# Order of the weight loads around the head outputs' read-back, in a two-layer attention and convolution trunk

## The chip, the cores and the metric

The kernel runs on one core of a Trainium2 chip. The metric is the device time of one execution in microseconds. Before the change three runs took 2350.84, 2352.64 and 2359.91 us; the median is 2352.64.

## The reference

Two layers of a diffusion trunk, over 512 latent tokens and 256 context tokens of width 1024. In each layer the tokens are normed and modulated, and one projection gives a convolution's input, queries, keys, values and gates. A convolution branch and a differential attention (8 heads, two softmax maps each) are projected, gated and merged, and a squared-ReLU MLP follows. Context tokens read only context tokens, and the last layer leaves their own update out. The part around the change:

```python
w = p[:, :, 0] - lam * p[:, :, 1]
out = rmsnorm(einsum('bhqk,bkhv->bqhv', w, vals), sub_g) * (1 - lam_init)   # per head
...
y_conv = conformer_conv(conv_in, ...) @ w_conv_out
y_attn = attn @ w_attn_out
g = sigmoid(gate_logits + b_gate)
return (g_conv * y_conv + g_attn * y_attn) @ w_out
```

The modulation is `silu(c) @ w_ada + b_ada`, six vectors of 1024 for the latent tokens and six for the context.

## The kernel before

All matrices are held with channels on the 128 partitions. To keep float32 accuracy each operand is split into a rounded half and a remainder (`split`, L75: ScalarE rounds at L76, VectorE or GpSimd subtracts at L77), and each product is three matmuls (`mm3`, L109 to L111: rounded by rounded, rounded by remainder, remainder by rounded).

Weights come in slabs of 256 columns, 1 MB each (`load_slab`, L84): a transfer on SyncE's queue (L90) into a tile of the tag `raw`, then the split, half a slab at a time, into the tags `whi` and `wlo`, two buffers each. In the stretch in question `raw` has two buffers, and the modulation's slabs (`ada_slab`, L217, transfer at L81) use the same two. A modulation slab needs no split: sixteen small matmuls (L224), a copy, two transposes (L233) and three small VectorE instructions. Layer 0 has 24 modulation slabs, of which 4 to 8 stand beside each stage; layer 1's were worked out earlier, in layer 0's MLP.

The attention writes each head's unnormed output to memory (`at_d`, L770) and, at its end, all the heads' scales (`rs_d`, L817). Both are read back: `branch_load` (L976) reads one latent head, or two context heads, into a tile `ar` of tag `t2k`, four buffers (L981), and its scales, spread over all partitions, into a tile `arb` of tag `ar`, three buffers (one transfer per head, L984); VectorE multiplies (L986). The loop at L1072 splits the product into `hh` and `hl` (`h1h` and `h1l` in the trace), in which the gates' input stood till then. Layer 0 has twelve such loads, eight latent heads and four pairs of context heads; layer 1 has the eight latent ones. The first four are traced ahead of the last gate slab.

The loop at L1077 then multiplies the heads by `w_attn_out`: four slabs, for each the load `wao`, in layer 0 also modulation slab 16 + s, then the matmuls `ya` of the latent and the context tokens (L1086). The layer norm of the convolution runs in pieces between the slabs.

The order on each engine is not the order of the code. A planner at build time takes instructions by their place in the code as their inputs and buffers come free in its own model of time, and writes each engine's list, which the chip runs in that order. `tc.issue_after(x)` adds an edge without a wait: what the block puts on `x`'s engine stands behind `x` in that engine's list, and nothing waits for `x` to finish.

Of the kernel before, what the change touches and what calls it, by code (L numbers as in the profile page):

```python
# [14 lines left out]
P = 128  # L15
# [36 lines left out]
def trunk_kernel(  # L52
# [6 lines left out]
    nc = tc.nc  # L59
# [15 lines left out]
    def split(hi, lo, src, lo_eng=None):  # L75
        nc.scalar.activation(out=hi, in_=src, func=AF.Copy)  # L76
        return (lo_eng or nc.vector).tensor_tensor(out=lo, in0=src, in1=f32(hi), op=ALU.subtract)  # L77

    def raw_slab(src, name):
        r = state["tp"].tile([P, KT, 256], F32, tag="raw", name=name, bufs=state["nraw"])  # L80
        nc.sync.dma_start(r, src)  # L81
        return r

    def load_slab(src, name, shape=(KT, 256), lo_eng=None):  # L84
        r = state["tp"].tile([P, *shape], F32, tag="raw", name=f"r_{name}", bufs=state["nraw"])
        if isinstance(src, (list, tuple)):
            for dst, s in src:
                nc.sync.dma_start(r[:, :, dst], s)
        else:
            state["load"] = nc.sync.dma_start(r, src)  # L90
        hi = wpool.tile([P, *shape], F32R, tag="whi", name=f"h_{name}")
        lo = wpool.tile([P, *shape], F32R, tag="wlo", name=f"l_{name}")
        half = shape[0] // 2
        engs = lo_eng if isinstance(lo_eng, tuple) else (lo_eng, lo_eng)
        with ExitStack() as behind:
            for ins in state["behind"]:
                behind.enter_context(tc.issue_after(ins))
            for n, (k, eng) in enumerate(zip((slice(0, half), slice(half, shape[0])), engs)):
                if n and state["turn"]:
                    behind.enter_context(tc.issue_after(state["turn"]))  # L100
                split(hi[:, k], lo[:, k], r[:, k], eng)
        return hi, lo

    def rows(src, col0, ncols):
        return src[:, col0 : col0 + ncols].rearrange("(k p) n -> p k n", p=P)
# [7 lines left out]
    def fm_block(ps, w, m0, a, toks, nk=KT, lo_last=False):  # L113

        if lo_last:
            for k in range(nk):
                for j in range(2):
                    nc.tensor.matmul(ps, w[j][:, k, m0 : m0 + P], a(k)[0][:, toks],
                                     start=k + j == 0, stop=False)
            for k in range(nk):  # L120
                nc.tensor.matmul(ps, w[0][:, k, m0 : m0 + P], a(k)[1][:, toks],
                                 start=False, stop=k == nk - 1)
            return
        for k in range(nk):
            mm3(ps, (w[0][:, k, m0 : m0 + P], w[1][:, k, m0 : m0 + P]),
                (a(k)[0][:, toks], a(k)[1][:, toks]), k == 0, k == nk - 1)
# [14 lines left out]
    rs_d = [dpool.tile([H, SEQ if i == DEPTH - 1 else NT], F32, name=f"rs_d{i}")  # L141
            for i in range(DEPTH)]

    state = {"behind": (), "turn": None}
# [72 lines left out]
    def ada_slab(i, L, s):  # L217

        mi = state["mi"]
        r = raw_slab(rows(w_ada[i], 256 * s, 256), f"ada{i}_{s}")  # L220
        ps = mi(f"adaps{i}_{s}")
        for k in range(KT):
            j = k % 4
            nc.tensor.matmul(ps[32 * j : 32 * j + 32, :256], cvec[:, k, :], r[:, k, :],  # L224
                             start=k < 4, stop=k >= 4, tile_position=(0, 32 * j))
        if state["nt"] == 3:
            sb = state["tp"].tile([P, 512], F32, tag="t2k", bufs=3, name=f"adasb{i}_{s}")[:, :256]
        else:
            sb = spool.tile([P, 512], F32, tag="dg", name=f"adasb{i}_{s}", bufs=1)[:, :256]
        nc.scalar.activation(out=sb, in_=ps[:, :256], func=AF.Copy)  # L230
        pc = ps[:, 256:512]
        for m in range(2):
            nc.tensor.transpose(pc[:, m * P : m * P + P], sb[:, m * P : m * P + P], ident)  # L233
        ad = L["ad"][:, :, 2 * s : 2 * s + 2]
        for q in range(2):
            nc.vector.tensor_reduce(
                out=ad[:, q], in_=pc.rearrange("p (m j r) -> p m j r", m=2, j=4)[:, :, :, q],
                axis=AX.X, op=ALU.add)
        nc.vector.tensor_tensor(
            out=ad, in0=ad,  # L240
            in1=L["cols"][:, R_BADA + 2 * s : R_BADA + 2 * s + 2].unsqueeze(1)
            .to_broadcast([P, 2, 2]),
            op=ALU.add)
# [126 lines left out]
    for t in range(NTT):  # L370
# [4 lines left out]
        if t == 1:  # L375
            L = layer_params(0)
# [72 lines left out]
    for i in range(DEPTH):  # L449
# [370 lines left out]
        def drain(gen):  # L820
            for _ in gen:
                pass
# [113 lines left out]
        def ps_for(g, name):  # L936
            if g.start:
                return mc.tile([P, 512], F32, tag="mc", name=name)
            return mm_tile(name)
# [28 lines left out]
        def some_taps(n):  # L968
            for _ in range(n):
                next(tap, None)  # L970
# [5 lines left out]
        def branch_load(h, g):  # L976
            W = g.stop - g.start
            per = 512 // W
            r = gp.tile([P, 512], F32, tag="t2k", bufs=4,
                        name=f"ar{i}_{h}_{g.start}").rearrange("p (h d) -> p h d", h=per)  # L980
            nc.sync.dma_start(r, at_d[i][h : h + per, :, g].rearrange("h p d -> p h d"))  # L981
            rb = gp.tile([P, 512], F32, tag="ar", bufs=3, name=f"arb{i}_{h}_{g.start}")
            for j in range(per):
                nc.sync.dma_start(rb[:, j * W : j * W + W],  # L984
                                  rs_d[i][h + j, g].partition_broadcast(P))
            nc.vector.tensor_tensor(out=r, in0=r, in1=rb.rearrange("p (h d) -> p h d", h=per),  # L986
                                    op=ALU.mult)
            ready.append(r)
# [3 lines left out]
        for half, lst in ((1, ga), (0, gc)):  # L992
            for s in range(4):
                if (half, s) not in wg:
                    gate_slab(half, s)
                if half == 0 and s == 3:
                    for hg in branch[:4]:
                        branch_load(*hg)
                w = wg.pop((half, s))
                for m in range(2):  # L1000
                    mb = 2 * s + m
                    t = g3(f"g{i}_{half}_{mb}")
                    lst[mb] = t
                    for g in groups:
                        W = g.stop - g.start
                        ps = ps_for(g, f"gt{i}_{half}_{mb}_{g.start}")
                        fm_block(ps[:, :W], w, m * P, lambda k: (hh[:, k], hl[:, k]), g)
                        bcol = R_BG + half * KT + mb
                        nc.scalar.activation(out=t[:, g], in_=ps[:, :W], func=AF.Sigmoid,
                                             bias=cols[:, bcol : bcol + 1])  # L1010
                    some_taps(per_gate)
                    if m == 0 and not state.get("ada_done"):
                        ada_slab(i, L, 8 + 4 * half + s)
# [61 lines left out]
            (h, g), r = branch.pop(0), ready.pop(0)  # L1075
            split(ah[:, h : h + r.shape[1], g], al[:, h : h + r.shape[1], g], r)
        for s in range(4):  # L1077
            w = load_slab(rows(w_attn_out[i], 256 * s, 256), f"wao{i}_{s}")
            if not state.get("ada_done"):
                ada_slab(i, L, 16 + s)  # L1080
            for g in groups:
                W = g.stop - g.start
                for m in range(2):
                    mb = 2 * s + m
                    ps = ps_for(g, f"ya{i}_{mb}_{g.start}")
                    fm_block(ps[:, :W], w, m * P, lambda k: (ah[:, k], al[:, k]), g)  # L1086
                    nc.vector.tensor_tensor(out=ga[mb][:, g], in0=ga[mb][:, g], in1=ps[:, :W],
                                            op=ALU.mult)
                    if last and (s, m) == (3, 0):
                        next(ln, None)  # L1090
                if s < 1 + last:
                    some_taps(per_ya)
            if s == last:
                drain(tap)
                ln = layer_norm()
            if s >= last:
                next(ln, None)
# [10 lines left out]
        for s in range(2):  # L1108
            state["behind"] = normed if s else ()
            w = load_slab(w_conv_out[i][:, 512 * s : 512 * s + 512]  # L1110
                          .rearrange("(k p) n -> p k n", p=P), f"wco{i}_{s}", shape=(CT, 512))
# [4 lines left out]
            for m in range(4):  # L1116
                mb = 4 * s + m
                for g in groups:
                    W = g.stop - g.start
# [186 lines left out]
        if not last:  # L1306
# [3 lines left out]
            L = Ln  # L1310
# [77 lines left out]
```

## Time and profile before

| | |
|---|---|
| median of three runs | 2352.64 us |
| profiled execution | 2353.61 us, span 2351.8 us |
| TensorE busy | 2276.6 us (97%) |
| VectorE, ScalarE, GpSimd busy | 1476.0, 995.2, 687.3 us |
| DMA | 224.76 MB, mean 96 GB/s |
| granted clock of TensorE, mean | 0.988 |

The span is the time from the first to the last instruction of the program; the profiled execution took 1.8 us more. In the rows, PE is TensorE, DVE is VectorE, ACT is ScalarE and SPq is SyncE's queue; L12 is line 12 of the kernel. `out<-in` names tiles without their numbers: `ar<-at_d` is a read of a head's output, `arb<-rs_d` one of its scales, `r_wao` an attention-output slab, `ada` a modulation slab. A transfer's row has the time that its issue took; the time to landing stands apart. The stage of the change lies from about 600 to 690 us in layer 0 and from about 1865 to 1910 us in layer 1.

### The profile page before, as it was taken

What the parts mean: (1) busy time and instruction counts of PE and PEld (TensorE: products, weight loads), DVE (VectorE), ACT (ScalarE), POOL (GpSimd) and SP (SyncE); (2) the same over time, 40 slices, a digit from 0 to 9 for tenths busy, and PEclk for the clock granted to TensorE, in tenths of its full rate; (3) what the DMA queues carried; (4) which work ended last, traced back from release to release, by engine and by line L of the source; (5) the groups of instructions that cost most, each with busy time, mean ns of one, the idle gap of its engine ahead of it and who ended that gap; (6) DMA issues with size and microseconds to landing.
All of it is one profiled execution on the core that took longest, in us unless ns stands there. A gap on an engine that the chain in (4) does not pass through costs nothing.

```text
span 2351.8 us, 36393 instructions
## 1 busy us (share of the span) xinstructions
PE 2276.6 (97%) x14626; PEld 2042.8 (87%) x14626; DVE 1476.0 (63%) x2587; ACT 995.2 (42%) x1965; POOL 687.3 (29%) x790
## 2 busy tenths in 40 slices
PE   7999999999999999999999999999899999999999
PEld 6999998888888988888888988999877879888887
DVE  6777776699656455565655465767759966433332
ACT  5556654522332362332415255655542334432432
POOL 1866764100000133232223266757610000000000
PEclk9999999999999999999999999999999999999999
DMA  9111111143535124333343211111114323223222
GB/s 313 57 42 34 44 46 44 46 160 125 180 119 175 51 81 127 115 128 115 113 130 127 89 46 57 44 43 44 61 59 141 112 90 126 90 90 98 99 90 72
DMA packets 222570, 224.76 MB, mean 96 GB/s; under 512 B 6256, under 2 KB 212544, under 8 KB 222272
## 3 DMA queue, kind: packets, MB, share of 16 engines
q1 hardware_dynamic: 222400, 222.43, 29.4%
q8 instruction: 115, 1.88, 0.3%
q14 instruction: 55, 0.45, 0.1%
HBM read 208.73 MB, written 13.67 MB: 95 GB/s over the span
## 4 chain that ended last, share of the span: by engine, by line
PE 83%; DVE 7%; ACT 4%; POOL 2%; DMA 2%; issue 1%; SPq 0%; ACTq 0%; POOLq 0%; DVEq 0%
PE r L109 6%; PE r L110 6%; PE r L111 6%; PE f L110 6%; PE f L109 6%; PE f L111 6%; PE gt L109 3%; PE gt L110 3%; PE gt L111 3%; PE qk L109 2%; PE qk L110 2%; PE qk L111 2%; PE v L109 2%; PE v L110 2%; PE v L111 2%; PE o L109 2%
## 5 line engine op out<-in xcount | busy, mean ns | idle before, releaser
L110 PE MATMUL f<-h2l,h_w 128*128 128x512 f32 (+1 forms) x832 | 284.5, 343 | 1.1 <-POOL h2l L77 1.1
L109 PE MATMUL f<-h2h,h_w 128*128 128x512 f32 (+1 forms) x832 | 282.9, 343 | 2.2 <-ACT h2h L76 1.7
L111 PE MATMUL f<-h2h,l_w 128*128 128x512 f32 (+1 forms) x832 | 283.0, 342 | 0.0
L109 PE MATMUL r<-fh,h_w 128*128 128x512 f32 (+1 forms) x832 | 283.0, 341 | 0.0
L110 PE MATMUL r<-fl,h_w 128*128 128x512 f32 (+1 forms) x832 | 282.9, 340 | 0.0
L111 PE MATMUL r<-fh,l_w 128*128 128x512 f32 (+1 forms) x832 | 282.8, 340 | 0.0
L77 POOL TENSOR_TENSOR l_w<-r_w,h_w 128x1024 fp32r<-128x1024 f32 x64 | 157.8, 2487 | 339.5 <-ACT h_w L76 339.5
L76 ACT ACTIVATE h_w<-r_w 128x1024 fp32r<-128x1024 f32 x128 | 128.6, 1052 | 254.3 <-PE r L110 117.2
L959 DVE SCALAR_TENSOR_TENSOR cacc<-z,cols,cacc 128x783 f32<-128x783 f32 (+1 forms) x240 | 201.2, 891 | 0.3
L279 DVE SCALAR_TENSOR_TENSOR adaac<-ar,cvec,adaac 128x256 f32<-128x256 f32 x336 | 160.8, 541 | 44.6 <-DMA ar<-in_w_ada_dram 22.7
L109 PE MATMUL qk<-h_wqk,h1h 128*128 128x256 f32 x640 | 183.3, 289 | 0.7 <-ACT h1h L76 0.7
L1154 DVE SCALAR_TENSOR_TENSOR X<-r,ad,X 128x512 f32<-128x512 f32 (+1 forms) x104 | 65.1, 625 | 189.0 <-PE r L111 188.8
L110 PE MATMUL qk<-l_wqk,h1h 128*128 128x256 f32 x640 | 180.6, 284 | 0.0
L111 PE MATMUL qk<-h_wqk,h1l 128*128 128x256 f32 x640 | 176.9, 285 | 0.3 <-POOL h1l L77 0.3
L726 DVE TENSOR_REDUCE st<-S 128x1 f32<-128x768 f32 (+1 forms) x160 | 134.7, 846 | 66.8 <-PE S L724 65.3
L109 PEld LDWEIGHTS f<-h2h,h_w 128*128 128x128 f32 x832 | 158.1, 191 | 21.1 <-ACT h2h L76 2.3
L110 PEld LDWEIGHTS f<-h2l,h_w 128*128 128x128 f32 x832 | 159.1, 191 | 19.6 <-POOL h2l L77 1.9
L111 PEld LDWEIGHTS f<-h2h,l_w 128*128 128x128 f32 x832 | 158.8, 191 | 17.7
L111 PEld LDWEIGHTS r<-fh,l_w 128*128 128x128 f32 x832 | 157.7, 190 | 17.7
L109 PEld LDWEIGHTS r<-fh,h_w 128*128 128x128 f32 x832 | 157.7, 190 | 17.4
L110 PEld LDWEIGHTS r<-fl,h_w 128*128 128x128 f32 x832 | 157.8, 190 | 17.2
L1235 DVE TENSOR_TENSOR fl<-fr,fh 128x512 fp32r<-128x512 f32 (+1 forms) x104 | 67.9, 659 | 138.4 <-ACT fr L1234 138.2
(255 smaller groups left out, 6297.7 us busy)
## 6 DMA issues: line engine op xcount, KB each, us to landing
r_w<-in_w_mlp_dram SPq DMA_DIRECT2D x64, 1024.0 KB, 5.4
ada<-in_w_ada_dram SPq DMA_DIRECT2D x24, 1024.0 KB, 6.1
ar<-in_w_ada_dram SPq DMA_DIRECT2D x48, 512.0 KB, 3.5
r_wqk<-in_w_in_dram SPq DMA_DIRECT2D x32, 512.0 KB, 5.1
r_wg<-in_w_in_dram SPq DMA_DIRECT2D x16, 1024.0 KB, 5.9
r_wv<-in_w_in_dram SPq DMA_DIRECT2D x8, 1024.0 KB, 5.2
r_wao<-in_w_attn_out_dram SPq DMA_DIRECT2D x8, 1024.0 KB, 4.8
r_wo<-in_w_out_dram SPq DMA_DIRECT2D x8, 1024.0 KB, 7.3
```

What stands on the lines that cost most here:

```text
L76: nc.scalar.activation(out=hi, in_=src, func=AF.Copy)
L77: return (lo_eng or nc.vector).tensor_tensor(out=lo, in0=src, in1=f32(hi), op=ALU.subtract)
L109: nc.tensor.matmul(ps, sh, mh, start=first, stop=False)
L110: nc.tensor.matmul(ps, sh, ml, start=False, stop=False)
L111: nc.tensor.matmul(ps, sl, mh, start=False, stop=last)
L279: nc.vector.scalar_tensor_tensor(out=a[:, q], in0=r[:, j], scalar=cvec[:, k, q : q + 1], in1=a[:, q], op0=ALU.mult, op1=ALU.add)
L726: nc.vector.tensor_reduce(out=st[:, m : m + 1], in_=S[:, :nkey], axis=AX.X, op=ALU.max, negate=True)
L959: nc.vector.scalar_tensor_tensor(out=ca[cc][:, :CV], in0=zt[cc][:, t : t + CV], scalar=wcol, in1=ca[cc][:, :CV], op0=ALU.mult, op1=ALU.add)
L1154: state["done"] = nc.vector.scalar_tensor_tensor(out=X[:, mb, g], in0=ps[:, :W], scalar=gate[:, s, mb : mb + 1], in1=X[:, mb, g], op0=ALU. ...
L1235: state["done"] = nc.vector.tensor_tensor(out=fl[mb][:, g], in0=r[:, :W], in1=f32(fh[mb][:, g]), op=ALU.subtract).ins
```

## The change

The last transfer of scales is remembered. In the loop over the four attention-output slabs, slab 1's transfer is placed behind it on SyncE's queue, and so are the modulation slabs 16 and 17 that stand beside slabs 0 and 1. In layer 1, which has no modulation slabs left, it is slab 1 alone. The edge holds for the transfers only, because no other instruction of the blocks runs on SyncE.

```diff
             for j in range(per):
-                nc.sync.dma_start(rb[:, j * W : j * W + W],
-                                  rs_d[i][h + j, g].partition_broadcast(P))
+                state["back"] = nc.sync.dma_start(rb[:, j * W : j * W + W],
+                                                  rs_d[i][h + j, g].partition_broadcast(P)).ins
...
         for s in range(4):
-            w = load_slab(rows(w_attn_out[i], 256 * s, 256), f"wao{i}_{s}")
+
+            with tc.issue_after(state["back"]) if s == 1 else ExitStack():
+                w = load_slab(rows(w_attn_out[i], 256 * s, 256), f"wao{i}_{s}")
             if not state.get("ada_done"):
-                ada_slab(i, L, 16 + s)
+                with tc.issue_after(state["back"]) if s < 2 else ExitStack():
+                    ada_slab(i, L, 16 + s)
```

## Rows read from the trace of the kernel before

**Rows 1.** The page: busy time, share of the span and instructions of each engine, and the chain that ended last by engine.

```profile
PE 2276.6 (97%) x14626; PEld 2042.8 (87%) x14626; DVE 1476.0 (63%) x2587; ACT 995.2 (42%) x1965; POOL 687.3 (29%) x790
...
PE 83%; DVE 7%; ACT 4%; POOL 2%; DMA 2%; issue 1%; SPq 0%; ACTq 0%; POOLq 0%; DVEq 0%
```

**Rows 2.** The waits of TensorE from 600 to 760 us (us in total, times, longest), which are this one row, and its timeline around it (start, us, instruction, idle before it and what ended that).

```profile
PE ya L109 <- ACT h1h L76: 2.2, 1, 2.2
...
648.25 0.28 PE L111 MATMUL ya<-h1h,l_wao 128*128 128x256 f32 x1
650.70 0.80 PE L109 MATMUL ya<-h1h,h_wao 128*128 128x256 f32 x2 [2.16 <-ACT h1h L76]
...
654.03 0.28 PE L109 MATMUL ya<-h1h,h_wao 128*128 128x256 f32 x1
...
654.84 0.79 PE L109 MATMUL ya<-h1h,h_wao 128*128 128x512 f32 x1
...
655.70 0.40 PE L111 MATMUL ya<-h1h,l_wao 128*128 128x512 f32 x1
```

**Rows 3.** Busy time of each engine in stretches: stretch, its length, PE, PEld, DVE, ACT and POOL busy (instructions), granted clock of TensorE, share of the DMA engines, GB/s.

```profile
636.00:648.25 12.25, 12.25 (x70) 10.69 (x69) 8.62 (x16) 1.90 (x3) 0.00 (x0) 1.00 0.97 302
650.56:653.98 3.42, 3.29 (x15) 3.29 (x16) 1.03 (x3) 0.08 (x1) 0.00 (x0) 0.50 0.00 0
653.98:657.40 3.42, 3.42 (x17) 2.55 (x16) 2.48 (x6) 2.93 (x4) 0.00 (x0) 1.00 0.00 0
```

**Rows 4.** The chain of waits from 620 to 660 us: start, us, what.

```profile
640.98 8.29 DMA ar<-at_d
...
650.01 0.64 ACT h1h L76
```

**Rows 5.** SyncE's queue in layer 0: start, us of the issue, transfer, how many.

```profile
623.87 0.37 SPq L90 DMA_DIRECT2D r_wao<-in_w_attn_out_dram  x1
...
636.35 0.38 SPq L81 DMA_DIRECT2D ada<-in_w_ada_dram  x1
638.64 1.27 SPq L984 DMA_DIRECT2D arb<-rs_d  x2
640.00 0.40 SPq L90 DMA_DIRECT2D r_wao<-in_w_attn_out_dram  x1
640.98 1.95 SPq L981 DMA_DIRECT2D ar<-at_d  x1
```

**Rows 6.** ScalarE's timeline in the same stretch.

```profile
632.79 1.99 ACT L76 ACTIVATE h_wao<-r_wao 128x1024 fp32r<-128x1024 f32 x2
634.69 0.46 ACT L1009 ACTIVATE g<-gt,cols 128x256 f32<-128x256 f32 x1
```

**Rows 7.** VectorE's timeline in the same stretch.

```profile
634.05 0.69 DVE L986 TENSOR_TENSOR ar<-ar,arb 128x512 f32<-128x512 f32 x1 [0.62 <-DMA arb<-rs_d]
...
635.26 1.22 DVE L77 TENSOR_TENSOR l_wao<-r_wao,h_wao 128x1024 fp32r<-128x1024 f32 x1
637.92 0.69 DVE L986 TENSOR_TENSOR ar<-ar,arb 128x512 f32<-128x512 f32 x1 [1.45 <-DMA ar<-at_d]
638.53 1.22 DVE L77 TENSOR_TENSOR l_wao<-r_wao,h_wao 128x1024 fp32r<-128x1024 f32 x1
...
640.27 1.29 DVE L77 TENSOR_TENSOR h1l<-ar,h1h 128x512 fp32r<-128x512 f32 x2
...
649.29 0.69 DVE L986 TENSOR_TENSOR ar<-ar,arb 128x512 f32<-128x512 f32 x1 [2.69 <-DMA ar<-at_d]
```

**Rows 8.** Time from issue to landing of a tile's transfers, in this order: the `ar` reads and the `arb` reads from 620 to 652 us, modulation slab 17 (issued at 636.35), and the two modulation slabs issued at 495.84 and 496.28.

```profile
DMA to landing us min/median/max: 4.0/4.6/8.3
DMA to landing us min/median/max: 3.4/4.6/6.2
DMA to landing us min/median/max: 8.6/8.6/8.6
DMA to landing us min/median/max: 5.4/6.6/7.9
```

**Rows 9.** TensorE's timeline where modulation slabs 16 and 17 are used (L224) and where slab 2's part of `ya` begins, and its one wait for a modulation slab's transfer in the whole span.

```profile
632.51 1.07 PE L224 MATMUL adaps<-ada,cvec 128*32 128x256 f32 x16
...
667.88 1.07 PE L224 MATMUL adaps<-ada,cvec 128*32 128x256 f32 x16
...
676.08 0.50 PE L109 MATMUL ya<-h1h,h_wao 128*128 128x512 f32 x1
...
PE adaps L224 <- DMA ada<-in_w_ada_dram: 0.2, 1, 0.2
```

**Rows 10.** Layer 1: the last `arb` on SyncE's queue, TensorE, weight loads and VectorE on `ya` during slab 0's part (as rows 3, for the instructions that name `ya` alone), and where slab 1's part begins.

```profile
1868.93 0.32 SPq L984 DMA_DIRECT2D arb<-rs_d  x1
...
1868.45:1879.80 11.35, 11.25 (x48) 8.52 (x47) 0.44 (x1) 1.00 0.48 159
...
1880.10 0.77 PE L109 MATMUL ya<-h1h,h_wao 128*128 128x512 f32 x1
...
1880.94 0.40 PE L111 MATMUL ya<-h1h,l_wao 128*128 128x512 f32 x1
```

**Rows 11.** A short wait of TensorE in layer 1, and the stretch around it as in rows 3.

```profile
1916.11 0.50 PE L118 MATMUL yc<-ch,h_wco 128*128 128x512 f32 x1 [0.94 <-ACT ch L1066]
...
1916.00:1926.00 10.00, 8.77 (x36) 6.58 (x37) 9.91 (x16) 5.48 (x9) 0.00 (x0) 1.00 0.23 76
```

## The prediction

> **What bounds the kernel now.** The page comes first: TensorE is busy for 97% of the span and holds 83% of the chain that ended last, so a change of queue order can only win time where TensorE stands still [rows 1]. The next view is TensorE's waits around the change in layer 0: from 600 to 760 us there is one, of 2.2 us, before `ya`, for ScalarE's `h1h` [rows 2]. The timeline gives its price: a 128x256 matmul starts every 0.12 us up to 648.25, the next starts at 650.70, so 2.45 - 0.12 = 2.33 us are lost. Then 15 matmuls take 650.70 to 654.03, 3.33 us in place of 15 x 0.12 = 1.80: 1.53 us more [rows 2]. The granted clock says why: 0.50 from 650.56 to 653.98 (1.2 GHz), 1.00 (2.4 GHz) afterwards [rows 3]. Together the stall costs 2.33 + 1.53 = **3.86 us**; from 654.84 on TensorE waits no more until 760.
>
> The chain of waits around it says who is late [rows 4]: 8.29 us of transfer `ar<-at_d`, the read of the last pair of context heads, then VectorE's product, ScalarE's rounding, and TensorE. SyncE's queue shows two causes [rows 5]. The read is issued at 640.98 only, and two 1 MB loads stand in front of it: a modulation slab (636.35, slab 17) and an attention-output slab (640.00, slab 2). The DMA engines are busy for 0.97 of 636 to 648.25 [rows 3], and where the heads' reads take 4.0 to 4.6 us from issue to landing at the least and the median, this one is the longest, 8.3 [rows 8]. It is issued late because its buffer is freed by the `h1l` that follows on VectorE at 640.27 (two of them in 1.29 us), while that head's product was done at 634.74: in between stand slab 1's rounding on ScalarE (632.79, 1.99 us) and its two remainders on VectorE (635.26 and 638.53, 1.22 us each) [rows 6, 7].
>
> **The change, part by part.** It adds no instruction and no wait on a semaphore; it moves three 1 MB transfers in layer 0 (slab 1 of attention-output, modulation slabs 16 and 17) and one in layer 1 (slab 1) on SyncE behind the last `arb`. GpSimd's queue is passed by none of them. What takes buffers of the same tag comes in traced order in the rows, so slab 2 and the later slabs follow too [rows 5].
>
> *What goes in layer 0.* Slab 1's split leaves the place between the head's product and its `h1l`. That head's rounding can then start when its product ends (634.74), and its `h1l` ends near 634.74 + 0.64 + 0.68 = 636.1 in place of 640.95 [rows 4, 7]. The last read goes out about 4.9 us earlier, with no 1 MB load queued before it, and lands after 4.0 to 6.2 us (the least head read, and the most of the `arb` group) [rows 8], at 640.1 to 642.3. The last `arb` was issued at 638.64 to 639.91 [rows 5]; if that stays, it lands at 642.6 to 645.0 (from 638.64 and the group's least, 3.4 would be 642.0; I take its median 4.6 from the end, 644.5). Product 0.69 and rounding 0.64 [rows 4, 7]: the rounded half is ready at about 645.9. TensorE wants it at 648.37, or at 647.3 when modulation slab 16's sixteen matmuls (632.51, 1.07 with the last one's drain) no longer stand ahead [rows 9]. Margin 1.4 us, so I take the stall as gone, 3.86 us won; the other end is 0, when the read still comes last.
>
> *What is late next in layer 0.* Slabs 16 and 1 now go out back to back after the last `arb`, from 639.91. The nearest row is the pair of modulation loads issued together at 495.84 and 496.28, which landed after 5.4 and 7.9 us [rows 8]. The second slab then lands at about 640.3 + 7.9 = 648.2. ScalarE's first half takes 1.05 (to 649.3), VectorE's 1.22 (to 650.5). TensorE reaches slab 1 at 654.84 - 3.86 = 650.98 and wants its remainder at the third matmul, 655.70 - 3.86 = 651.84 [rows 2]. Covered by 1.3 us; with one other VectorE product in front (0.69) by 0.6. If the landing takes 8.6, as slab 17 did [rows 8], no cover is left. Cost 0 to 1.5 us; I take 0. Slab 16's matmuls cost the same wherever they stand. Slab 17 has long slack: it landed at 645.0 (636.35 + 8.6) and was used at 667.88 [rows 5, 8, 9]. Slab 2 is wanted when its part of `ya` begins, 676.08 - 3.9 = 672.2 [rows 9], some 20 us after a buffer comes free near 652.
>
> The Trainium skill speaks against this part: "Trainium Kernel Development and Optimization", section Best Practices, asks for double buffering so that transfers lie beside compute. The lead of slab 1 falls here from 31 us (623.87 to 654.84) to 10.7 (640.3 to 651.0), and load and first half's split take 7.9 + 1.05 + 1.22 = 10.2 by the rows. Followed strictly, the rule would leave slab 1 where it is and the sum at 0; the trace shows the early slab idle until 632.79, so only the last part of that lead does work.
>
> *Layer 1.* TensorE is busy for 11.25 of the 11.35 us of slab 0's part of `ya` [rows 10]: 0.1 to win at most, left out. Slab 1 moves from well ahead of the heads' reads to behind the last `arb` at 1868.93 [rows 10], with slab 2 right behind it. As first of a pair it lands 5.4 us later, near 1874.7 (as second, 7.9: 1877.2). Its rounding (1.05) and remainder (1.22, one product of 0.69 in front) end at 1877.7 to 1880.2; TensorE wants the slab at 1880.10, its remainder at 1880.94 [rows 10]. Covered; 0 to 1.5 us, I take 0. VectorE is not relieved, its work only changes place.
>
> Sum: the profiled execution took 2353.61 us (span 2351.8 and 1.8 around it); 2353.61 - 3.86 = 2349.75. It lies 0.97 above the median of the runs, 2352.64, so the median to expect is 2348.8, written 2349. In the profile the span should be 2347.9.
>
> **Rivals.** *The wait stays.* The edge is tied to the last `arb`, and before the change the last `arb` (638.64) went out ahead of the last read (640.98) [rows 5]. If it does so again, slabs 16 and 1 stand in front of the read just as 17 and 2 did, and it lands near 648. For it: the order in the rows. Against: what held the read back was slab 1's split, which is gone, and 636.1 lies before the product at 637.92 that frees the `arb`'s buffer [rows 7], by 1.8 us. A mixture, a shorter stall without the low clock or a short wait for slab 1, ends here too. Result 0 to -2: 2352.
>
> *The wait moves to what was pushed back (slower).* Engines run their lists in a fixed order. If slab 16's matmuls, or slab 1's, stand in TensorE's list where the planner took them as landed, TensorE waits for them in the middle of `ya`, and nothing else can pass. How far plan and chip differ is seen in VectorE's waits for transfers in this stretch: 0.62, 1.45 and 2.69 us [rows 7]. At 2.69 with the low clock's 1.53 one such wait costs 4.2, and one in each layer 8.4, against 3.9 won: +4.5, or 2357. It decides from a single wait of 2.3 us on. Against it: of TensorE's waits on DMA for such slabs in the whole kernel there is one, of 0.2 us [rows 9], and a short one left the clock alone (0.94 us at 1916, with 1.00 granted there [rows 11]).
>
> *It does something else.* A planner that lists the whole program anew may shift later work either way. Nothing in the rows prices that; I leave it a small chance.
>
> **How the numbers follow.** Forecast (stall gone, 2347 to 2351): 0.50. Wait stays or a short one takes its place (2351 to 2353): 0.29. Wait moves, slower (2353 to 2358): 0.17. Elsewhere: 0.04. The three runs of before lie from 2350.84 to 2359.91, so a median can stray by some us on its own. Range 2344 to 2358. Faster or slower by over 0.5% (11.8 us, about what a measurement of this kernel can tell from no change) would need times below 2340.9 or above 2364.4: no case but the last reaches there. Faster 0.04, within 0.93, slower 0.03.
>
> **What would show it.** Right: SyncE issues the last `ar<-at_d` of layer 0 near 636, before the last `arb`, then slab 16 and slab 1; `h1l` of the last latent head follows its rounding at once; no TensorE wait for `h1h` in `ya`, and a clock of 1.00 from 600 to 760; slab 2 of `ya` starts some 3.9 us earlier. Wrong: a wait before `ya` on `h_wao` or `l_wao`, or on `ada` at L224, in either layer; a last read still landing near 649; or a span that differs although this stretch is as told.

## The result and the profile after

The changed kernel takes 2357.47 us (median of 22 runs, 2354.1 to 2361.82); the kernel before takes 2353.34 us beside it (22 runs, 2346.99 to 2359.91). The ratio is 1.002, interval 1.0012 to 1.0027: slower by 0.2%, some 4 us (2.8 to 6.4 by the interval), where 2349 and a gain had been forecast. The time lies inside the range of the prediction, near its upper end; the change went the other way than forecast, and the likeliest case did not come.

The page of the kernel after, first the span, then the engines' busy time as in [rows 1]:

```profile
span 2356.2 us, 36394 instructions
...
PE 2280.6 (97%) x14626; PEld 2045.1 (87%) x14626; DVE 1488.6 (63%) x2587; ACT 996.1 (42%) x1965; POOL 687.3 (29%) x790
```

TensorE does the same 14626 matmuls and is busy for 4.0 us more: part of the loss is low clock, which the page counts as busy. The page cannot say where. TensorE's waits can: first those from 600 to 760 us, then those from 1860 to 1900 us (us in total, times, longest).

```profile
PE adaps L224 <- DMA ada<-in_w_ada_dram: 1.7, 1, 1.7
PE adaps L233 <- ACT adasb L230: 0.7, 1, 0.7
...
PE ya L109 <- ACT h1h L76: 1.7, 1, 1.7
PE ya L109 <- DVE g L1090: 0.9, 1, 0.9
PE ya L110 <- DVE h1l L77: 0.8, 1, 0.8
```

In layer 0 the wait for the head's `h1h` [rows 2] has gone and two others stand in its place, both for modulation slab 16. In layer 1, where there was no wait in this stretch, there are three.

SyncE's queue after the change, in layer 0 and then in layer 1, answers to [rows 5]:

```profile
637.82 0.37 SPq L981 DMA_DIRECT2D ar<-at_d  x1
638.24 0.46 SPq L984 DMA_DIRECT2D arb<-rs_d  x1
638.75 0.42 SPq L81 DMA_DIRECT2D ada<-in_w_ada_dram  x1
639.37 0.43 SPq L90 DMA_DIRECT2D r_wao<-in_w_attn_out_dram  x1
...
1867.70 0.32 SPq L984 DMA_DIRECT2D arb<-rs_d  x1
1868.07 12.57 SPq L90 DMA_DIRECT2D r_wao<-in_w_attn_out_dram  x3
```

The change does what it says: slab 16 and slab 1 follow the last `arb`, and the last read of a head goes out 3.2 us earlier than at 640.98 [rows 5] (4.0 us earlier, when both are counted from the last gate product on TensorE). In layer 1 three slabs' loads are folded into one row; slabs 1 and 2 go out together, from 1868.07. Before, slab 1 (at 1850.65) and slab 2 went out well ahead of the last `arb` at 1868.93 [rows 10]:

```profile
1850.65 11.25 SPq L90 DMA_DIRECT2D r_wao<-in_w_attn_out_dram  x2
```

**Layer 0, TensorE.** The timeline of the kernel after (idle before and what ended it in brackets):

```profile
644.78 0.28 PE L111 MATMUL ya<-h1h,l_wao 128*128 128x256 f32 x1
646.77 1.07 PE L224 MATMUL adaps<-ada,cvec 128*32 128x256 f32 x16 [1.71 <-DMA ada<-in_w_ada_dram]
...
651.85 0.44 PE L233 MATMUL adaps<-cst,adasb 128*128 128x128 f32 x2 [0.70 <-ACT adasb L230]
```

Slab 16's sixteen matmuls stood ahead of `ya` before, at 632.51 [rows 9]. Now the planner has put them into the middle of the context heads' part. The view has no landing time for this slab; the weight load that waits for it starts at 646.74, so it landed some 8 us after its issue. Their copy on ScalarE comes late in its turn, because it stands behind slab 1's rounding in that engine's list:

```profile
643.79 0.64 ACT L76 ACTIVATE h1h<-ar 128x512 fp32r<-128x512 f32 x1 [0.60 <-DVE ar L986]
649.52 2.01 ACT L76 ACTIVATE h_wao<-r_wao 128x1024 fp32r<-128x1024 f32 x2 [5.09 <-DMA r_wao<-in_w_attn_out_dram]
651.43 0.37 ACT L230 ACTIVATE adasb<-adaps 128x256 f32<-128x256 f32 x1
```

**Layer 1.** TensorE, ScalarE and VectorE of the kernel after:

```profile
1879.37 0.73 PE L109 MATMUL ya<-h1h,h_wao 128*128 128x512 f32 x2 [1.66 <-ACT h1h L76]
1880.90 0.80 PE L110 MATMUL ya<-h1l,h_wao 128*128 128x512 f32 x1 [0.80 <-DVE h1l L77]
...
1883.89 0.80 PE L109 MATMUL ya<-h1h,h_wao 128*128 128x512 f32 x1 [0.91 <-DVE g L1090]
...
1876.79 2.00 ACT L76 ACTIVATE h_wao<-r_wao 128x1024 fp32r<-128x1024 f32 x2 [5.76 <-DMA r_wao<-in_w_attn_out_dram]
1878.70 0.61 ACT L76 ACTIVATE h1h<-ar 128x512 fp32r<-128x512 f32 x1
...
1873.70 0.69 DVE L986 TENSOR_TENSOR ar<-ar,arb 128x512 f32<-128x512 f32 x1 [0.86 <-DMA arb<-rs_d]
...
1877.88 2.36 DVE L77 TENSOR_TENSOR l_wao<-r_wao,h_wao 128x1024 fp32r<-128x1024 f32 x2 [1.68 <-ACT h_wao L76]
1880.16 0.68 DVE L77 TENSOR_TENSOR h1l<-ar,h1h 128x512 fp32r<-128x512 f32 x1
1880.76 2.47 DVE L1035 SCALAR_TENSOR_TENSOR cacc<-ln,cacc 128x512 f32<-128x512 f32 x4
1883.16 1.27 DVE L1090 TENSOR_TENSOR g<-g,ya 128x512 f32<-128x512 f32 x2
```

Read the ScalarE rows first. The last head's product on VectorE ends at 1874.39, and its rounding could follow; but slab 1's rounding stands ahead of it in ScalarE's list, and that waits 5.76 us for a slab that lands at 1876.71, 8.6 us after its issue. So the head's `h1h` runs at 1878.70, its `h1l` at 1880.16 behind slab 1's remainder, and slab 0's eviction `g` (the instruction that takes slab 0's result from TensorE and frees its buffer there) at 1883.16 behind four layer-norm instructions. In the kernel before, the same instructions stand in another order: slab 1's rounding ran early among the heads, and the evictions stood ahead of the four:

```profile
1868.27 2.01 ACT L76 ACTIVATE h_wao<-r_wao 128x1024 fp32r<-128x1024 f32 x2 [1.86 <-PE gt L110]
...
1879.36 1.28 DVE L1087 TENSOR_TENSOR g<-g,ya 128x512 f32<-128x512 f32 x2 [0.69 <-PE ya L111]
1880.68 2.48 DVE L1035 SCALAR_TENSOR_TENSOR cacc<-ln,cacc 128x512 f32<-128x512 f32 x4
```

After the change TensorE has no wait for slab 1 itself: it waits for the head, the head's remainder and the eviction, 1.66 + 0.80 + 0.91 = 3.37 us in all. Most of the rest of layer 1's loss is the granted clock, which was at its lower level of 1.2 GHz for a part of this time (columns as in [rows 3]; the first row is layer 0):

```profile
646.70:656.00 9.30, 8.53 (x67) 7.17 (x68) 4.38 (x10) 2.41 (x4) 0.00 (x0) 1.00 0.68 221
...
1880.40:1884.20 3.80, 2.39 (x5) 1.49 (x6) 3.80 (x7) 2.25 (x3) 0.00 (x0) 0.51 0.75 256
1884.20:1888.00 3.80, 3.80 (x11) 3.00 (x11) 3.69 (x5) 1.95 (x4) 0.00 (x0) 0.60 0.15 33
```

In layer 1 it is 0.51 and 0.60 in the two stretches of 3.8 us; in layer 0 it stays at 1.00. The kernel before has 1.00 at this place in layer 1.

**The account.** The stretch of the change is counted from the start of the last gate product to the first convolution-output product, on TensorE. Before: 632.30 to 714.45, and 1868.07 to 1916.11. After: 633.16 to 714.09, and 1866.83 to 1921.17. Layer 0 takes 80.93 us in place of 82.15 (1.22 won), layer 1 takes 54.34 in place of 48.04 (6.30 lost). What lies ahead, between and behind differs by +0.86, -0.88 and -0.65 in these two executions. Together +4.4, as the spans do (2356.2 against 2351.8).

### The profile page after: what moved, and what is told of

The parts are those of the page before. It is cut to its first block, busy times and chain, and to the rows that moved or that the text cites. A ratio compares the mean times of both kernels' runs of the same rounds, so it can differ in the third digit from the quotient of the medians.

```text
span 2356.2 us, 36394 instructions
## 1 busy us (share of the span) xinstructions
PE 2280.6 (97%) x14626; PEld 2045.1 (87%) x14626; DVE 1488.6 (63%) x2587; ACT 996.1 (42%) x1965; POOL 687.3 (29%) x790
## 4 chain that ended last, share of the span: by engine, by line
PE 82%; DVE 8%; ACT 3%; DMA 2%; POOL 2%; issue 1%; SPq 0%; ACTq 0%; POOLq 0%; DVEq 0%
PE r L109 6%; PE r L110 6%; PE r L111 6%; PE f L110 5%; PE f L109 5%; PE f L111 5%; PE gt L109 3%; PE gt L111 3%; PE gt L110 3%; PE qk L109 2%; PE qk L110 2%; PE qk L111 2%; PE v L109 2%; PE v L110 2%; PE v L111 2%; PE o L109 2%
## 5 line engine op out<-in xcount | busy, mean ns | idle before, releaser
L279 DVE SCALAR_TENSOR_TENSOR adaac<-ar,cvec,adaac 128x256 f32<-128x256 f32 x336 | 167.5, 561 | 43.4 <-DMA ar<-in_w_ada_dram 22.0
L1238 DVE TENSOR_TENSOR fl<-fr,fh 128x512 fp32r<-128x512 f32 (+1 forms) x104 | 72.8, 706 | 127.9 <-ACT fr L1237 127.6
```

The costliest lines, as they stand in the source:

```text
L279: nc.vector.scalar_tensor_tensor(out=a[:, q], in0=r[:, j], scalar=cvec[:, k, q : q + 1], in1=a[:, q], op0=ALU.mult, op1=ALU.add)
L1238: state["done"] = nc.vector.tensor_tensor(out=fl[mb][:, g], in0=r[:, :W], in1=f32(fh[mb][:, g]), op=ALU.subtract).ins
```

## The experiments

For all of them, the stretch in each layer as counted above (from the one profiled execution of each kernel), and the median of the runs. Each ratio is to runs of the kernel before taken beside it: their medians are 2353.00 us for e1 to e4, 2353.58 for e5 to e7 and 2351.26 for e8 and e9. The expectations count the stretch from the first `ya` product instead: that is 0.2 us less in layer 1 and 1.2 less in layer 0 (0.1 less where slab 16's matmuls, 1.07 us, have moved behind that point).

| kernel | layer 0, us | layer 1, us | median, us | ratio to before, interval |
|---|---|---|---|---|
| before | 82.15 | 48.04 | 2353.34 | |
| the change | 80.93 | 54.34 | 2357.47 | 1.0012 to 1.0027 |
| e1, layer 0 alone | 81.77 | 48.39 | 2350.27 | 0.998 to 1.0 |
| e2, layer 1 alone | 83.03 | 53.15 | 2357.38 | 1.0012 to 1.0035 |
| e3, slab 1 in layer 0 alone | 78.67 | 48.05 | 2347.47 | 0.997 to 0.999 |
| e6, slabs 1 and 16 in layer 0 | 80.71 | 47.86 | 2350.72 | 0.9974 to 1.0002 |
| e4, no edge on a transfer, slab 1's split late | 79.06 | 50.76 | 2351.47 | 0.9983 to 1.0005 |
| e7, the same in layer 0 alone | 79.09 | 48.26 | 2348.72 | 0.9974 to 1.0 |
| e5, the change, slab 1's split late | 82.13 | 54.16 | 2357.91 | 1.0002 to 1.0032 |
| e8, evictions first in layer 1 | 78.29 | 48.40 | 2348.85 | 0.9979 to 0.9997 |
| e9, layer 1 behind the fifth head | 78.51 | 52.12 | 2354.99 | 0.9997 to 1.0016 |

The table also shows how far one profile can be trusted. Where a layer is left as it was, its stretch repeats within 0.9 us: 82.15 and 83.03 in layer 0, 47.86 to 48.39 in layer 1. The stretch between the two layers, which no edit names, took from 1151.3 to 1156.1 us. So the whole span of one execution cannot price an edit of 3 us; the stretch can. The profiled execution is not always a typical one: that of e9 is the fastest of its 11 runs, 6.7 us below their median, and that of e2 lies 4.3 above.

**e1: the change in layer 0 alone.**

```diff
-            with tc.issue_after(state["back"]) if s == 1 else ExitStack():
+            with tc.issue_after(state["back"]) if s == 1 and not last else ExitStack():
...
-                with tc.issue_after(state["back"]) if s < 2 else ExitStack():
+                with tc.issue_after(state["back"]) if s < 2 and not last else ExitStack():
```

> The three edges of layer 0 kept, the one of layer 1 undone. Theory A (the loss is made in layer 1, where ScalarE has slab 1's rounding in its list ahead of the last head's and waits for slab 1's transfer): the waits of 1.66, 0.80 and 0.91 us before ya near 1880 are gone and the time falls to 1 us below before (ratio 0.999 to 1.000), because layer 0 itself won 1.2 us in the trace of after. Theory B (the loss is not tied to layer 1, but to a different fall of TensorE's low clock after the waits in between, as at 829 us): the time stays 3 to 5 us above before (ratio 1.0015 to 1.002).

2350.27 us (11 runs). Layer 1 falls back to 48.39, so its loss comes from its own edge and from nothing that layer 0 does. In layer 0 the wait for slab 16 stays, and here the granted clock is lower after it (0.60 from 645.10 to 649.00):

```profile
645.11 1.22 PE L224 MATMUL adaps<-ada,cvec 128*32 128x256 f32 x16 [1.99 <-DMA ada<-in_w_ada_dram]
```

**e2: the change in layer 1 alone.**

```diff
+            with tc.issue_after(state["back"]) if s == 1 and last else ExitStack():
...
+                with tc.issue_after(state["back"]) if False else ExitStack():
```

> The edge of layer 1 kept, those of layer 0 undone. Theory A: 5 to 6 us above before (ratio 1.002 to 1.0027), with slab 1's transfer landing some 8.6 us after its issue and ScalarE idle until then while the last head's product is ready. Theory B: within 1 us of before.

2357.38 us (12 runs): the whole loss of the change, from one moved transfer. Layer 0 has its old wait for `h1h` (3.1 us in this execution), layer 1 three waits with the same names as after the change (0.5, 0.8 and 1.8 us). Slab 1 landed 7.4 us after its issue here, not 8.6.

**e3: slab 1 in layer 0 alone, modulation slabs free.**

```diff
+            with tc.issue_after(state["back"]) if s == 1 and not last else ExitStack():
...
+                with tc.issue_after(state["back"]) if False else ExitStack():
```

> Layer 0 alone, and there only slab 1 of attention-output is queued behind the last arb (modulation slab 17 follows it, since it takes its buffer in traced order); slab 16 stays where it was. Theory A: TensorE no longer waits for slab 16 (1.71 us) nor for its copy behind slab 1's rounding (0.70); slab 1 has no 1 MB transfer ahead and lands about 5 us after its issue near 639, so ya goes through without a wait: 3 to 4 us below before (ratio 0.9983 to 0.9988). Rival (slab 1 itself is late in layer 0 too): no better than e1_layer0_only, 0 to 1 us below before.

2347.47 us (11 runs), ratio 0.998, interval 0.997 to 0.999: faster than the kernel before, and the lowest median and ratio of all, though the intervals of e7 and e8 overlap this one. It is near the 2349 that the prediction's sum gave for the whole change. TensorE has no wait at all from 600 to 760 us. SyncE's queue and ScalarE show why:

```profile
618.25 0.37 SPq L81 DMA_DIRECT2D ada<-in_w_ada_dram  x1
...
637.42 0.37 SPq L981 DMA_DIRECT2D ar<-at_d  x1
637.84 0.46 SPq L984 DMA_DIRECT2D arb<-rs_d  x1
638.39 0.39 SPq L90 DMA_DIRECT2D r_wao<-in_w_attn_out_dram  x1
638.87 0.65 SPq L81 DMA_DIRECT2D ada<-in_w_ada_dram  x1
...
645.13 0.63 ACT L76 ACTIVATE h1h<-ar 128x512 fp32r<-128x512 f32 x1 [2.68 <-DVE ar L986]
647.37 2.01 ACT L76 ACTIVATE h_wao<-r_wao 128x1024 fp32r<-128x1024 f32 x2 [1.60 <-DMA r_wao<-in_w_attn_out_dram]
```

Slab 16 goes out at 618.25 and its matmuls stand ahead of `ya` as before. Slab 1 lands some 8.9 us after its issue (by the end of ScalarE's wait; 5 had been expected) and is still in time: in ScalarE's list its rounding stands behind the last head's, not ahead. 82.15 - 78.67 = 3.48 us are won, against 3.86 reckoned for the stall.

**e6: slab 16 as well, slab 17 free.** Slab 16 or slab 17, which takes the gain back?

```diff
+                with tc.issue_after(state["back"]) if s == 0 and not last else ExitStack():
```

> In layer 0 slab 1 and modulation slab 16 behind the last head outputs, slab 17 and layer 1 as before. Theory A (slab 16, whose products stand early in TensorE's list, is what takes back most of layer 0's gain): a wait of 1.5 to 2.5 us for the modulation slab near 645 us, layer 0's stretch 81 to 82 us, as with both modulation slabs moved, and 2350 to 2351. Theory B (slab 17 does it, by holding back slab 2 or by its own landing): no such wait, the stretch 77.5 to 78.5 us and 2347 to 2348, as with slab 1 alone moved.

2350.72 us (12 runs). Slab 16: both waits are there again (1.56 us for its landing, 0.6 for its copy), and layer 0 goes from e3's 78.67 to 80.71 (by the expectation's way of counting 80.6, just under the 81 to 82 of theory A). Slab 17, free here, makes no difference that shows against the change's 80.93.

**e4: no edge on a transfer, slab 1's split later in the lists.** Does the last read come late because of the queue, or because slab 1's split holds back the buffer it needs? Here no transfer gets an edge; slab 1's rounding and remainder are put behind those of the last heads.

```diff
-            split(ah[:, h : h + r.shape[1], g], al[:, h : h + r.shape[1], g], r)
+            state["heads"] = (
+                nc.scalar.activation(out=oh, in_=r, func=AF.Copy).ins,
+                nc.vector.tensor_tensor(out=ol, in0=r, in1=f32(oh), op=ALU.subtract).ins)
...
+            state["behind"] = state["heads"] if s == 1 else ()
             w = load_slab(rows(w_attn_out[i], 256 * s, 256), f"wao{i}_{s}")
+            state["behind"] = ()
```

> No transfer moved: the kernel before, with slab 1's split (rounding on ScalarE, remainder on VectorE) put in their lists behind the split of the last head, in both layers. Theory C (in layer 0 the last read was late because slab 1's split held back the instruction that frees its buffer): the last read goes out near 638 and ahead of slab 17, TensorE's wait of 2.16 us goes, 3 to 4 us below before (ratio 0.9983 to 0.9988), layer 1 unchanged. Rival D (it was late because 1 MB transfers stood in front of it): the wait of before stays, ratio 1.000.

2351.47 us (11 runs), which the interval does not tell from before. The two layers go opposite ways, and theory C missed the second. Layer 0 gains 3.1 us: the last read goes out at 638.36 with slab 1 fetched as early as ever. Slab 17 and slab 2 now go out behind it (slab 2 at 651.31), without any edge on them.

```profile
638.36 0.38 SPq L981 DMA_DIRECT2D ar<-at_d  x1
...
640.86 0.38 SPq L81 DMA_DIRECT2D ada<-in_w_ada_dram  x1
```

Layer 1 loses 2.7. TensorE waits 2.91 us there until 1879.23, and VectorE's rows show the likely reason, which is not the one that the wait's name gives:

```profile
1879.23 0.47 PE L109 MATMUL ya<-h1h,h_wao 128*128 128x512 f32 x1 [2.91 <-ACT csq L1041]
...
1873.74 2.35 DVE L77 TENSOR_TENSOR l_wao<-r_wao,h_wao 128x1024 fp32r<-128x1024 f32 x2
1876.01 2.48 DVE L1035 SCALAR_TENSOR_TENSOR cacc<-ln,cacc 128x512 f32<-128x512 f32 x4
1878.40 1.27 DVE L1092 TENSOR_TENSOR g<-g,ya 128x512 f32<-128x512 f32 x2
```

TensorE stands still from 1876.3 on. Slab 1's data came long ago here, no transfer is late, and still slab 0's evictions run at 1878.40 only, behind slab 1's remainder and four layer-norm instructions. (`csq`, which the row names, ends at 1879.2; so does the first eviction, within 0.15. The matmul does not read `csq`; it needs the buffer that the eviction frees.) So the lists cost here by themselves. It is not the split's place alone: its remainder ends at 1876.09, and had the evictions come next, TensorE would have waited about half a us (an estimate: the first eviction takes 0.69, and TensorE was free at 1876.3). The four layer-norm instructions, 2.48 us together, stood behind the evictions in the kernel before. With the split moved the planner listed them ahead, and it did the same in the change, e2, e5 and e9, that is wherever slab 1's transfer or split was moved in layer 1 and no edge held them back.

**e7: the same in layer 0 alone.** The condition becomes `s == 1 and not last`.

> All transfers in the order of the kernel before; in layer 0 alone slab 1's rounding and subtraction put behind those of the last head outputs on ScalarE and VectorE. Theory A (in layer 0 the head's wait comes from slab 1's split, which holds the buffer of the last load, and not from the queue as such; in layer 1 the split is better where it was): layer 0's stretch near 77.9 us against 80.9, layer 1's 47.8 as before, the time 2349 to 2350.5. Theory B (the transfers' order is what has to change): layer 0's stretch 80 us or more and the time within 1 us of before.

2348.72 us (12 runs), layer 0 at 79.09 and layer 1 at 48.26. Almost all of e3's gain in the stretch is to be had without an edge on a transfer. It was the place of slab 1's split in two lists, ahead of the `h1l` that frees the buffer, that made the last read go out late. Then it also stood behind two 1 MB loads and took 8.3 us to land [rows 8], against 5.0 here. No run has the one without the other, so their shares are not shown.

**e5: the change, with slab 1's split behind the heads' in both layers.** The edit of e4 on top of the change.

> The change as it stands, and slab 1's rounding and subtraction put behind those of the last head outputs in ScalarE's and VectorE's lists, in both layers. Theory A, lists (layer 1 loses because slab 1 lands late, near 1876.7 us, and the last head's two instructions stand behind its rounding and subtraction in lists of fixed order): the waits of TensorE for the last head go, a shorter one for slab 1 itself stays, and layer 1 from the first attention-output product to the first convolution-output product takes 50 to 51.5 us against 54.1 with the change and 47.8 before; layer 0 keeps the wait of 1.7 us for the modulation slab 16, so the time is 2353 to 2355. Theory B, landing alone (slab 1 is simply too late for its own products, whatever the lists say): layer 1 keeps 53 to 54 us and the time stays at 2356 to 2358.

2357.91 us (12 runs): the time is what theory B gave, and theory A's number was a miss. But B's reason is wrong too. The trace of layer 1:

```profile
1882.03 0.47 PE L109 MATMUL ya<-h1h,h_wao 128*128 128x512 f32 x1 [4.39 <-DVE g L1095]
...
1874.64 0.69 DVE L1079 TENSOR_TENSOR h1l<-ar,h1h 128x512 fp32r<-128x512 f32 x1
1876.53 2.36 DVE L77 TENSOR_TENSOR l_wao<-r_wao,h_wao 128x1024 fp32r<-128x1024 f32 x2 [1.21 <-ACT h_wao L76]
1878.81 2.48 DVE L1035 SCALAR_TENSOR_TENSOR cacc<-ln,cacc 128x512 f32<-128x512 f32 x4
1881.20 1.28 DVE L1095 TENSOR_TENSOR g<-g,ya 128x512 f32<-128x512 f32 x2
```

The head is no longer late: its `h1l` runs at 1874.64, and slab 0's products end near 1877.6. Then TensorE waits for the buffer that slab 0's eviction frees, and the eviction stands on VectorE behind slab 1's remainder and the four layer-norm instructions. Slab 1's remainder is ready from 1878.89 on, 3.1 us before TensorE goes on. Three waits have become one; the loss is the same (54.16 against 54.34).

**e8: slab 0's evictions ahead of the layer norm in layer 1.** Slab 1's transfer as in the change, the modulation slabs free, the split behind the heads in layer 1, and one more edge on VectorE:

```diff
+                    with tc.issue_after(state["evict"]) if last else ExitStack():
+                        nc.vector.scalar_tensor_tensor(out=dd, in0=mu[:, :W], scalar=-1.0 / CW,
+                                                       in1=dd, op0=ALU.mult, op1=ALU.add)
```

> Slab 1's transfer behind the last head outputs in both layers, as in the change; the modulation slabs free. In layer 1, in the lists, slab 1's split behind the last head's split, and the four layer-norm subtractions (the ones that read the mean out of ln) behind slab 0's two evictions. In the run with the split alone moved TensorE waited 4.4 us for an eviction that stood behind slab 1's remainder and these four. Theory A, lists (the late landing costs by what stands behind slab 1's split on VectorE, not by slab 1's own lateness): that wait falls to 1 to 2 us, layer 1's stretch to 49.5 to 51.5 us against 53.9, layer 0's stays near 77.5 as with slab 1 alone moved there, and the time is 2348.5 to 2351. Theory B, landing (slab 1 itself, landing 8 us behind its issue, is what TensorE waits for): the wait changes its name to slab 1's remainder but not its size, layer 1's stretch stays at 53 to 54 us and the time at 2353 to 2354.

2348.85 us (11 runs; before 2351.26 beside it), layer 1 at 48.40. The edge brings back the order of the kernel before, evictions first. The wait is down to 0.6 us:

```profile
1875.55 2.35 DVE L77 TENSOR_TENSOR l_wao<-r_wao,h_wao 128x1024 fp32r<-128x1024 f32 x2
1877.82 1.27 DVE L1096 TENSOR_TENSOR g<-g,ya 128x512 f32<-128x512 f32 x2
1879.02 2.47 DVE L1036 SCALAR_TENSOR_TENSOR cacc<-ln,cacc 128x512 f32<-128x512 f32 x4
```

In this execution the late transfer costs nearly nothing: 5.8 of e5's 6.1 us of loss in layer 1 are gone, more than theory A had forecast. But part of that is luck, because slab 1 landed 6.9 us after its issue here and 8.9 in e5. Counted from the last gate product, its remainder starts 1.7 us earlier than in e5; with e5's landing TensorE would have waited 0.55 + 1.74 = 2.3 us, by an estimate from these rows. So of the 3.8 us by which the wait fell, about 2.1 belong to the order of VectorE's list and 1.7 to the landing. The low clock that followed e5's wait (0.57 from 1882 to 1886) and is missing here (1.00) cannot be shared out between them.

**e9: layer 1's slab behind the fifth of eight heads.** How much of the delay does it take?

```diff
+            with tc.issue_after(state["ar1_4"] if last else state["back"]) if s == 1 else ExitStack():
```

> Slab 1 behind the last head outputs in layer 0, and in layer 1 only behind the fifth of the eight head outputs: about 3.8 us earlier there than in the change, among the last four head outputs, and so landing near 1872 to 1873 on the axis of the run with the change, with those reads slower for it. Theory A (layer 1's loss follows slab 1's landing through the lists that wait for it): layer 1's stretch between 48 and 51 us, and 2347.5 to 2350.5. Theory B (any place among or behind the reads costs what the change costs): 53 to 54 us, 2353 or more.

2354.99 us (11 runs, 2348.31 to 2356.48), ratio 1.0006, interval 0.9997 to 1.0016: between the two theories and no answer to the question. The stretch of 52.12 comes from the fastest of these runs. The edge did something else besides: both slabs went out among the last four heads' reads, whose last one took 7.8 us to land, and two of TensorE's waits are for the `h1l` of heads that came late (2.2 us together). It looks like layer 0's old trouble, brought into layer 1.

## Why the prediction was wrong

**The stall and its cause: right.** That slab 1's split held back the buffer of the last read is seen in e4 and e7, and that this read would go out ahead of the last `arb` in the trace after. The step "I take the stall as gone, 3.86 us won" measured 3.48 us where it stands alone (e3).

**"Slab 16's matmuls cost the same wherever they stand": wrong.** Sixteen matmuls take 1.07 us in both places, but their place in a fixed list decides what waits with them. They stood where TensorE came to them 1.7 us before the slab landed (that the planner's own model had it landed by then is likely, but its times are not on record), and the copy of their result stood behind slab 1's rounding. 1.71 + 0.70 = 2.41 us of the 3.5 went back. The prediction sized landing times for slab 1 and slab 17 and none for slab 16's new place.

**Slab 1 in layer 0, "Cost 0 to 1.5 us; I take 0": right.** TensorE has no wait for `h_wao` or `l_wao` after the change, nor in e3 or e6.

**Layer 1, "Covered; 0 to 1.5 us, I take 0": the step that failed.** It cost 6.3 us (5.1 in e2). Two things were wrong in it. The landing was taken from the first of a pair of modulation slabs, 5.4 us [rows 8], and came after 8.6. That alone was not fatal: the first half of slab 1 was rounded by 1877.85 and its remainder done by about 1879.1, and with nothing else late TensorE would have wanted them at 1878.86 and 1879.70 on this trace (the times of [rows 10], less the 1.24 us by which the last gate product came earlier). The larger error is what the cover was measured against: the time at which TensorE wants slab 1. The first to suffer were the instructions that stand behind slab 1's split in ScalarE's and VectorE's lists, the last head's `h1h` and `h1l` and slab 0's evictions, which TensorE wants earlier. "VectorE is not relieved, its work only changes place" named the move and did not follow it: before, slab 1 had been in memory for 13 us when its split ran at 1868.27 between the heads, and its rounding waited for no transfer; after, the same instruction waits for one, with the last head behind it. And the planner changed one order that the prediction could not read from the rows of before: the four layer-norm instructions went ahead of the evictions. e5 and e8 show this by size: with the head put first the wait went to the next victim, the eviction, and the loss stayed; with that put first too, the wait fell from 4.4 to 0.6 us, of which some 1.7 is the earlier landing. e4 shows the same victim without any late transfer.

**The rivals.** "The wait moves to what was pushed back" is what happened, in both layers, at 2357 against 2357.47. Its mechanism, "engines run their lists in a fixed order", was right; in layer 0 it was slab 16's matmuls in TensorE's list, in layer 1 not slab 1's matmuls, as the rival had it, but ScalarE's and VectorE's lists ahead of them. Its price was 4.2 us in each layer; the measured losses were 2.4 in layer 0 (no low clock) and 6.3 in layer 1 (3.37 of waits, most of the rest low clock), so it is luck that the totals nearly meet. It had 0.17, for two reasons. The first was that the kernel before has only one wait on DMA for such a slab [rows 9]: that says how well the lists suited the old arrival times, and nothing about new ones. The second, that a short wait leaves the clock alone [rows 11], held in layer 0 and not after the three waits of layer 1.

**On the skill's rule.** The Trainium skill ("Trainium Kernel Development and Optimization", Best Practices) asks for double buffering so that transfers lie beside compute. In layer 1 the trace agrees: slab 1 went out some 19 us later (counted from the last gate product), work came to wait for its transfer, and 6.3 us were lost. Layer 0 does not speak against it, but shows that a longer lead is not better by itself: in e3 slab 1 went out some 14 us later, its transfer still lay beside compute, and 3.5 us were won. By these traces it was not the lead that told the two apart, but what stood behind the split in the lists.

**What stays open.** How much of layer 1's loss is the low clock was read from the timeline and not tried. Where slab 1 was moved in layer 1, slab 2 followed close behind it, so whether slab 1 alone would land sooner there was not tried either. Why the planner lists slab 1's split ahead of the last head in layer 1 and behind it in layer 0, and why it moved the layer norm, was not looked into. That what the replanning moved elsewhere costs nothing is only bounded: the stretch between the layers varies by some 5 us over the profiles, and with one profile of each kernel it cannot be said how much of that is the execution and how much the plan.

## What to carry to other kernels

When a transfer is moved later, look at the instruction that consumes it on each in-order engine, and price what stands behind that instruction, not only the final user of the data. An edge on a queue changes arrival times, and a planner that lists the program anew may then set instructions in another order that the edge does not name, so compare the lists of every engine before and after. In these traces a late slab cost nothing where its consumer stood behind the heads in the lists (e3), and it cost waits where the heads, the evictions or a modulation slab's copy stood behind its consumer. Where one edit covers several places, test them one at a time: here one of four moved transfers brought all of the gain, and two of the others the loss.

## What the hardware showed beside this

The length of a wait alone did not tell whether the granted clock is lower after it. Near 828 us both kernels have the same wait of 1.84 us for `dg_n`; from 827 to 833 the first row is of the kernel before, the second of the kernel after:

```profile
827.00:833.00 6.00, 4.72 (x38) 4.70 (x39) 5.13 (x12) 4.08 (x12) 1.80 (x2) 1.00 0.58 178
```

```profile
827.00:833.00 6.00, 5.08 (x28) 5.06 (x29) 4.41 (x11) 3.49 (x10) 1.43 (x2) 0.72 0.55 175
```

In the stretches of the change the granted clock stayed at 1.00 (2.4 GHz) after waits of 1.56 (e6), 1.71 (after) and 2.91 us (e4, layer 1), and was 0.60, 0.50, 0.74 and 0.57 in the stretches that follow those of 1.99 (e1), 2.16 (before), 2.33 and 4.39 us (both e5); the values between 0.50 and 1.00 are means over stretches with both levels.

A 1 MB load with a second one queued behind it landed after 6.9 to 8.9 us in layer 1 (8.6 after the change, 7.4 in e2, 8.9 in e5, 6.9 in e8) and the second after 11.0 (after the change), where the modulation pair in [rows 8] took 5.4 and 7.9 and slab 1 before the change took 4.8.
